# Feed-forward tiles: the up-projection one tile further ahead, and the second half of an operand's making in two pieces

## The chip, the cores and the metric

The kernel runs on one core of a Trainium2 chip. The metric is the device time of one execution in microseconds; less is better. PE is the matrix engine (TensorE), DVE the vector engine, ACT the scalar engine, POOL and SP issue transfers here.

## The reference, cut to what matters

A stream of 528 columns (16 learned tokens, 512 frames) of width 1024 goes through two layers in float32. Each has a mixer (retention in the first, latent attention in the second) and a feed-forward part; the change is in the feed-forward part alone:

```python
def swiglu(hn, w1, w3, w2):
    return (jax.nn.silu(hn @ w1) * (hn @ w3)) @ w2

for layer in range(DEPTH):
    ...
    h = h + swiglu(rmsnorm(h, norm_ffn_g[layer]), ffn_w1[layer], ffn_w3[layer], ffn_w2[layer])
```

`w1` and `w3` are 1024 x 2816, `w2` is 2816 x 1024.

## The kernel before

**Split values.** A float32 matrix is used as a high part `hi` (a copy to the matmul's type, made by ACT) and a residue `lo` (the value less `hi`, made by DVE). `split` issues the two, one after the other, and the residue waits for the copy. Each product takes three matmuls per block: `hi hi`, `hi lo`, `lo hi`.

**Tiles and periods.** The feed-forward part is a sequence of tiles (`seq`). A tile up (`Up`) takes 128 columns of `w1` and of `w3`, a tile down (`Down`) 2 x 128 columns of `w2` over one part of the 22 hidden blocks. The hidden blocks go in inner pairs: tiles up 2j and 2j+1 give pair j, of which the operand `xp` of the tiles down is made. Most tiles are multiplied in Strassen's manner, with seven products of half blocks (Q1 to Q7) for eight; the first two or three tiles up and the last part down are plain. A tile up has four blocks in each product (12 matmuls), a tile down of the first three parts three blocks (9 matmuls).

`PARTS = (3, 3, 3, 2)` are the inner pairs of the four parts. Tiles up of the first two parts run two tiles beyond those that the part needs (L1059, the `+ 2`), then come the part's four tiles down. So the sequence of 38 tiles is: up 0 to 7, down 8 to 11, up 12 to 17, down 18 to 21, up 22 to 29, down 30 to 33, down 34 to 37 (plain).

**A period** (`period(i)`, L911) issues the work of tile i = `q`, of its predecessor `prev`, and the preparation for `nxt` = i+1 and `far` = i+2. PE's order is Q1 of `q`, Q7 and Q3 of `prev`, Q5, Q2 and Q6 of `q`, Q4 of `prev`. All engines run their instructions in the order in which the code issues them. For DVE that is, in a period: the `wlo` of `group2(q)`, the `wlo4` of `group4(prev)` (names of a kind drop their digits in the profile: `wlo<-raw,whi` with 512 columns), what `hidden(i)` issues, `combine(prev)` (`b<-b,t`), two multiplications of `prev.mid` (`t<-a,r`, `t<-b,r`), `sum2(nxt)` (`raw<-raw`, L856), the `wlo` of `group(q, q.r3, ...)`, the `wlo` of `group1(nxt)`, `sum4(nxt)`, and two instructions of `prev.fin`. Each `wlo` has its `whi` on ACT, in the same order. The next period's Q1 needs the `wlo` of `group1(nxt)`.

**The operands of a pair** (`operands`, L784) are made in two steps by a generator. The first makes the parts of Q1, Q2 and Q3 and two differences `e<-e`; the second makes two more `e<-e`, and then splits all four into the parts of Q5, Q7, Q4 and Q6 (`xp<-e` on ACT, 4 x 264 columns, and the residue `xp<-e,xp` on DVE). `hidden(i)` (L1072) issues one step per period: the first step of the next pair if its values are there and a buffer is free, the second step in the period after. The list `room` holds the buffers with the period from which each is free: three at once for the first part, the same three from one period after the first part's last tile down for the second part (P13), and so on. So first steps fall on the periods 3, 5, 7, then 13, 15, 17, then 23, 25, 27, second steps on 4, 6, 8, then 14, 16, 18, then 24, 26, 28; the plain operands of the last part are made in 31 and 33.

```python
        def hidden(i):
            if rest:
                drain(rest.pop())
            elif len(ops) < len(hid) and i >= room[len(ops)][1]:
```

Of the kernel before, what the change touches and what calls it, by code (L numbers as in the profile page):

```python
# [11 lines left out]
F32 = mybir.dt.float32  # L12
# [3 lines left out]
ALU = mybir.AluOpType  # L16
# [19 lines left out]
KH = HID // P  # L36
# [11 lines left out]
PARTS = (3, 3, 3, 2)  # L48
# [3 lines left out]
Q1, Q2, Q3, Q5, Q7, Q4, Q6 = range(7)  # L52
# [10 lines left out]
def drain(steps):  # L63
    for _ in steps:
        pass
# [195 lines left out]
class Kernel:  # L261
# [522 lines left out]
    def operands(self, pool, vv, w, b12=None):  # L784


        xp = pool.tile([P, 7, 2, HT], F32R, tag="xp", name=self.name("xp"))
        (b11, b12_), (b21, b22) = ((vv[:, i, :w], vv[:, i, w : 2 * w]) for i in range(2))
        for q, z in ((slice(Q1, Q3), vv[:, :, :w]), (Q3, b22)):
            self.split(xp[:, q, 0, :w], xp[:, q, 1, :w], z)  # L790
        if b12 is not None:
            self.split(*b12, b12_)
            yield xp
        self.tt(b11, b11, b12_, ALU.subtract)
        self.tt(b12_, b22, b12_, ALU.subtract)
        if b12 is None:
            yield xp
        self.tt(b22, b22, b11, ALU.add)
        self.tt(b21, b22, b21, ALU.subtract)
        if b12 is not None:  # L800
            yield
        self.split(xp[:, Q5:, 0, :w], xp[:, Q5:, 1, :w], self.blocks(vv, w))

    @staticmethod
    def blocks(vv, w):
# [8 lines left out]
    def quads(self, seq, first, w, ready, also, hidden):  # L814
# [15 lines left out]
        def load1(q):  # L830
            q.r1 = f3(q, raw(q))
            nc.sync.dma_start(out=q.r1, in_=f3(q, q.src[:, : 2 * q.n]))

        def load3(q):
            q.r3 = f3(q, raw(q))
            nc.sync.dma_start(out=q.r3[:, 0], in_=q.part(1))

        def load2(q):
            q.r2 = f3(q, raw(q))
            if q.plain:  # L840
                nc.sync.dma_start(out=q.r2, in_=f3(q, q.src[:, 2 * q.n :]))
            else:
                nc.sync.dma_start(out=q.r2[:, 1], in_=q.part(2))
# [5 lines left out]
        def add1(q):  # L849
            nc.gpsimd.dma_start(out=q.r1[:, 1], in_=q.part(3), accum_op=ALU.add)  # L850

        def add3(q):
            nc.gpsimd.dma_start(out=q.r3[:, 0], in_=q.part(0), accum_op=ALU.add)
# [17 lines left out]
        def group1(q):  # L871
            group(q, q.r1, *((A11, A21) if q.plain else (Q1, Q5)))

        def group2(q):
            group(q, q.r2, *((A12, A22) if q.plain else (Q6, Q2)))
# [6 lines left out]
        def product(q, bank, p, first):  # L882
            wt = q.f[p]
            for k, xp in enumerate(q.xs()):
                cs = slice(k * P, (k + 1) * P)
                for i, (u, v) in enumerate(((0, 0), (0, 1), (1, 0))):
                    nc.tensor.matmul(bank, wt[u][:, cs], xp[:, p, v, :w], start=first and k == 0 and i == 0,  # L887
                                     stop=False, skip_group_check=True)

        def plain(q, j, k, of=((0, 0), (0, 1), (1, 0), (1, 1))):  # L890

            cs = slice(k * P, (k + 1) * P)
            xs = q.blocks(k)[2 * j : 2 * j + 2]
            for row, col in of:
                wt, x = q.f[((A11, A12), (A21, A22))[row][j]], xs[col]
                bank = ((q.a, q.b), (q.d, q.c))[row][col]
                for i, (u, v) in enumerate(((0, 0), (0, 1), (1, 0))):
                    nc.tensor.matmul(bank, wt[u][:, cs], x[v], start=j == 0 and k == 0 and i == 0,  # L898
                                     stop=False, skip_group_check=True)
# [11 lines left out]
        def period(i):  # L911
            q, nxt, far = (seq[j] if j < len(seq) else None for j in range(i, i + 3))
            prev = seq[i - 1] if i else None
            mixed = lambda z: z is not None and not z.plain
            on = lambda place: [f() for f in also.get((i, place), ())]
            if q:
                a, ps = self.banks[i % 2]
                q.a, (q.b, q.d, q.c), q.ps = a[:, :w], (ps[:, j, :w] for j in range(3)), ps[:, :, :w]
            if i == 0:
                load1(far)  # L920
                group1(nxt)
                if mixed(far):
                    add1(far)
                    load3(far)
                load2(far)
                if mixed(far):
                    add3(far)
                on("start")
                for k in range(len(q.xs())):
                    plain(q, 0, k)  # L930
                    plain(q, 1, k)
                    on(k)
                return
            pairs = range(len(q.xs())) if q else ()
            if mixed(q):
                product(q, q.a, Q1, True)
            elif nxt:

                for of in ((0, 1), (1, 0), (1, 1), (0, 0)) if i == 1 else ((0, 0), (0, 1), (1, 0), (1, 1)):
                    for k in pairs:  # L940
                        plain(q, 0, k, (of,))
            if q:
                group2(q)
                on("group2")
                if far and i < first:
                    load1(far)
                if mixed(q):
                    nc.scalar.copy(out=q.b, in_=q.a)
            if mixed(far):
                add1(far)  # L950
            if mixed(prev):
                group4(prev)
            if mixed(q):
                load4(q)
            hidden(i)
            if mixed(prev):
                product(prev, prev.d, Q7, False)
                product(prev, prev.b, Q3, False)
                combine(prev)
            prev.mid(prev.a, prev.b)  # L960
            on("mid")
            if mixed(nxt):
                sum2(nxt)
            if mixed(q):
                group(q, q.r3, Q7, Q3)
            if mixed(far):
                load3(far)
            if mixed(q):
                product(q, q.c, Q5, True)
            elif nxt:  # L970
                for k in pairs:
                    plain(q, 1, k)
            else:
                for row in range(2):
                    for k in pairs:
                        for j in range(2):
                            plain(q, j, k, ((row, 0), (row, 1)))
            if mixed(q):
                q.q5 = self.temp()[:, :w]
                nc.scalar.copy(out=q.q5, in_=q.c)  # L980
            if nxt:
                group1(nxt)
                if far:
                    load2(far)
                if i >= first - 1 and i + 3 < len(seq):
                    load1(seq[i + 3])
            if mixed(nxt):
                sum4(nxt)
            on("group1")
            if mixed(q):  # L990
                product(q, q.a, Q2, False)
                product(q, q.b, Q6, False)
                nc.scalar.copy(out=q.d, in_=q.b)
            prev.act()
            if mixed(prev):
                product(prev, prev.d, Q4, False)
            prev.fin(prev.ps[:, 1:3])
            if mixed(far):
                add3(far)
            on("end")  # L1000
# [12 lines left out]
    def ffn(self, layer, full):  # L1013
# [4 lines left out]
        w = HT if full else SEQ // 2  # L1018
# [37 lines left out]
        hid, ops, seq, room = [], [], [], []  # L1056
        m = 0
        for part, size in enumerate(PARTS):
            end = min(2 * sum(PARTS[: part + 1]) + 2, KH) if part < 2 else KH  # L1059
            while m < end:  # L1060
                seq.append(Up(self, a[f"w13_{layer}"][m], KD // 2, m < PLAIN[layer], m, x, hid, w))
                m += 1
            if part == 2:
                room += [(self.xp, len(seq) + 1)] * 2
            for o in range(KD // 2):
                seq.append(Down(self, a[f"w2_{layer}_{part}"][o], size, part == 3, o, ops, sum(PARTS[:part]), full))
            if part < 2:
                room += [(self.hp, len(seq) + 1)] * 3
        room = [(self.hp, 0)] * 3 + room
        rest = []  # L1070

        def hidden(i):  # L1072
            if rest:
                drain(rest.pop())
            elif len(ops) < len(hid) and i >= room[len(ops)][1]:
                make = self.operands if len(ops) < sum(PARTS[:3]) else self.plain_operands
                rest.append(make(room[len(ops)][0], hid[len(ops)], w))
                ops.append(next(rest[0]))

        self.quads(seq, PLAIN[layer], w, self.ready, also, hidden)  # L1080
        self.shut("hp", "xp", "wx")
# [325 lines left out]
```

## Time and profile before

| | us |
|---|---|
| median of 3 runs | 1473.9 (1472.87 to 1476.27) |
| the profiled execution | 1473.63 |
| its span | 1471.9 |
| feed-forward of layer 0 (in the span) | 465.90 to 819.50 |
| feed-forward of layer 1 | 1105.50 to 1455.20 |

Over the span PE is busy 97%, DVE 77%, ACT 50%, POOL 9%. In the two feed-forward stretches DVE is busy 310.33 of 353.60 us and 303.52 of 349.70 us. The share of busy time says little about which engine sets the end: PE's matmuls overlap, and DVE's share is a mean over periods with and without operands to make. So what is to be read are the few places at which a matmul starts late, and what it waited for.

### The profile page before, as it was taken

Reading aid. Unit: us, or ns where it says so; the run is one execution under the profiler, and the core shown is the slowest. Engines: PE = TensorE matmul, PEld = TensorE weight load, DVE = VectorE, ACT = ScalarE, POOL = GpSimd, SP = SyncE. Lnnn points to the kernel's source line nnn. Section 1 sums busy time; section 2 is a strip of 40 time slices with the busy share of each in tenths; the row PEclk is TensorE's granted clock in tenths of the full one; section 3 lists DMA queues with packets and bytes.
Section 4 is the critical chain, followed back from the end, with each engine's and each line's share of the span. In section 5 each row is a group of like instructions: output and inputs, shape, how many; then the busy total and the mean of one; then the engine's idle time right before and its main releaser. Section 6 shows DMA issues by size and latency. Waiting matters only on the chain.

```text
span 1471.9 us, 27735 instructions
## 1 busy us (share of the span) xinstructions
PE 1422.8 (97%) x11088; PEld 1376.7 (94%) x11088; DVE 1131.2 (77%) x1823; ACT 736.9 (50%) x1299; POOL 129.7 (9%) x170
## 2 busy tenths in 40 slices
PE   8999999999999999999999999989999999999995
PEld 8999999999999999999999989778989999999995
DVE  7665566566568998988987877567788988989876
ACT  5452442342356555555554534565556655555552
POOL 2000000000000111111110000110000112121100
PEclk9999999999999999999999999999999999999998
DMA  6213223123113767768764232311113768677651
GB/s 213 91 48 103 69 70 101 58 73 101 59 58 94 179 161 184 177 147 205 179 151 136 100 96 72 104 51 55 58 58 100 189 157 200 162 190 188 162 139 65
DMA packets 77314, 176.80 MB, mean 120 GB/s; under 512 B 8944, under 2 KB 24432, under 8 KB 77184
## 3 DMA queue, kind: packets, MB, share of 16 engines
q1 hardware_dynamic: 56592, 138.76, 29.6%
q0 software_dynamic: 20592, 36.26, 14.1%
q8 instruction: 87, 1.43, 0.4%
q14 instruction: 43, 0.35, 0.1%
HBM read 171.57 MB, written 2.10 MB: 118 GB/s over the span
## 4 chain that ended last, share of the span: by engine, by line
PE 73%; DVE 18%; ACT 3%; issue 3%; DMA 2%; DVEq 0%; ACTq 0%; POOLq 0%
PE ps L371 22%; PE b L887 16%; PE ps L373 8%; DVE wlo L331 7%; PE ps L638 6%; PE a L887 6%; PE b L898 4%; PE ps L721 2%; DVE xp L331 2%; DVE t L331 2%; DVE e L331 2%; PE ps L679 2%; PE ps L116 2%; DMA raw<-w 1%; ACT xp L335 1%
## 5 line engine op out<-in xcount | busy, mean ns | idle before, releaser
L335 ACT CAST whi<-raw 128x1024 fp32r<-128x1024 f32 (+4 forms) x402 | 347.6, 869 | 275.6 <-PE ps L371 137.8
L887 PE MATMUL b<-xp,whi 128*128 128x264 f32 (+1 forms) x2280 | 417.2, 283 | 5.6 <-DVE xp L331 3.6
L331 DVE TENSOR_TENSOR wlo<-raw,whi 128x1024 fp32r<-128x1024 f32 (+4 forms) x402 | 389.9, 995 | 40.1 <-ACT whi L335 37.3
L887 PEld LDWEIGHTS b<-xp,whi 128*128 128x128 f32 x2280 | 351.4, 188 | 7.7 <-DVE xp L331 4.4
L887 PE MATMUL b<-xp,wlo 128*128 128x264 f32 (+1 forms) x1140 | 321.7, 282 | 0.0
L371 PE MATMUL ps<-s,whi 128*128 128x264 f32 x1824 | 300.9, 287 | 9.4 <-ACT whi L335 6.7
L371 PEld LDWEIGHTS ps<-s,whi 128*128 128x128 f32 x1824 | 255.3, 190 | 11.7 <-ACT whi L335 6.7
L887 PEld LDWEIGHTS b<-xp,wlo 128*128 128x128 f32 x1140 | 214.2, 188 | 0.0
L371 PE MATMUL ps<-s,wlo 128*128 128x264 f32 x912 | 186.4, 286 | 0.0
L887 PE MATMUL a<-xp,whi 128*128 128x264 f32 (+1 forms) x912 | 170.4, 283 | 0.0
L371 PEld LDWEIGHTS ps<-s,wlo 128*128 128x128 f32 x912 | 142.4, 190 | 0.1
L887 PEld LDWEIGHTS a<-xp,whi 128*128 128x128 f32 x912 | 140.6, 188 | 0.0
L887 PE MATMUL a<-xp,wlo 128*128 128x264 f32 (+1 forms) x456 | 130.5, 286 | 8.0 <-DVE wlo L331 8.0
L850 POOL DMA_DIRECT2D raw<-w x63 | 54.6, 867 | 805.9 <-DMA raw<-w 428.6
L373 PE MATMUL ps<-s,whi 128*128 128x512 f32 x368 | 119.0, 405 | 3.4 <-ACT t L127 3.4
L638 PE MATMUL ps<-whi,s 128*128 128x256 f32 x640 | 116.5, 281 | 0.3 <-DVE s L331 0.3
L638 PEld LDWEIGHTS ps<-whi,s 128*128 128x128 f32 x640 | 99.1, 188 | 0.6 <-PE ps L118 0.3
L331 DVE TENSOR_TENSOR s<-ps,s 128x256 fp32r<-128x256 f32 (+3 forms) x88 | 46.6, 546 | 65.3 <-ACT s L335 50.8
L887 PEld LDWEIGHTS a<-xp,wlo 128*128 128x128 f32 x456 | 85.7, 188 | 11.8 <-DVE wlo L331 11.6
L638 PE MATMUL ps<-wlo,s 128*128 128x256 f32 x320 | 89.5, 280 | 0.0
L373 PEld LDWEIGHTS ps<-s,whi 128*128 128x128 f32 x368 | 68.6, 192 | 18.0 <-ACT t L127 3.5
L331 DVE TENSOR_TENSOR xp<-e,xp 128x528 fp32r<-128x528 f32 (+5 forms) x82 | 64.1, 808 | 22.9 <-ACT xp L335 22.7
(178 smaller groups left out, 2088.2 us busy)
## 6 DMA issues: line engine op xcount, KB each, us to landing
raw<-w SPq DMA_DIRECT2D x133, 256.0 KB, 3.7
raw<-w SPq DMA_DIRECT2D x49, 512.0 KB, 5.2
raw<-w POOLq DMA_DIRECT2D x78, 256.0 KB, 5.4
raw<-w SPq DMA_DIRECT2D x72, 192.0 KB, 2.9
raw<-w SPq DMA_DIRECT2D x24, 384.0 KB, 4.4
raw<-w POOLq DMA_DIRECT2D x48, 192.0 KB, 4.0
raw<-w_v SPq DMA_DIRECT2D x16, 512.0 KB, 3.7
raw<-w_g SPq DMA_DIRECT2D x16, 512.0 KB, 3.5
```

Source lines behind the costliest of these rows:

```text
L116: nc.tensor.matmul(out, x[:, qs], y[:, cs], start=t == 0, stop=t == 4 and not masked)
L331: self.nc.vector.tensor_tensor(out=out, in0=a, in1=b, op=op)
L335: self.nc.scalar.copy(out=hi, in_=src)
L371: mm(ps[:, h * 512 : h * 512 + HT], w[p], x[q][:, h * HT : (h + 1) * HT], start=s, stop=e)
L373: mm(ps[:, :SEQ], w[p], x[q], start=s, stop=e)
L638: mm(ps[:, :256], x[k][p][:, c], w[k][q], start=k == 0 and i == 0, stop=k == last and i == 2)
L679: nc.tensor.matmul(ps[:n, half * 512 : half * 512 + HT], k[d][p][:, t0 : t0 + n], q[d][s][:, half * HT : (half + 1) * HT], start=i == 0, s ...
L721: mm(out, v[j][p][:, c], s[:, c0 : c0 + HT], start=j == 0 and i == 0, stop=False)
L850: nc.gpsimd.dma_start(out=q.r1[:, 1], in_=q.part(3), accum_op=ALU.add)
L887: nc.tensor.matmul(bank, wt[u][:, cs], xp[:, p, v, :w], start=first and k == 0 and i == 0, stop=False, skip_group_check=True)
L898: nc.tensor.matmul(bank, wt[u][:, cs], x[v], start=j == 0 and k == 0 and i == 0, stop=False, skip_group_check=True)
```

## The change

Three things. The tiles up of the first two parts run three tiles beyond those that the part needs, not two. In the second step of `operands`, a `yield` stands between the copy and the residue when an inner pair's operands are made (`b12 is None`; with `b12`, at the start of a layer, nothing changes). And `hidden` is called at three places of a period: a first step is issued where it was (place 1, behind `group4`); of a second step the two differences and the copy are issued ahead of `group4` (place 0), the residue behind `prev.mid` (place 2).

```diff
@@ operands
         self.tt(b22, b22, b11, ALU.add)
         self.tt(b21, b22, b21, ALU.subtract)
+        hi, lo, vv = xp[:, Q5:, 0, :w], xp[:, Q5:, 1, :w], self.blocks(vv, w)
         if b12 is not None:
             yield
-        self.split(xp[:, Q5:, 0, :w], xp[:, Q5:, 1, :w], self.blocks(vv, w))
+        self.nc.scalar.copy(out=hi, in_=vv)
+        if b12 is None:
+            yield
+        self.tt(lo, vv, hi.bitcast(F32), ALU.subtract)
@@ period
             if mixed(far):
                 add1(far)
+            hidden(i, 0)
             if mixed(prev):
                 group4(prev)
             if mixed(q):
                 load4(q)
-            hidden(i)
+            hidden(i, 1)
             if mixed(prev):
                 product(prev, prev.d, Q7, False)
                 product(prev, prev.b, Q3, False)
                 combine(prev)
             prev.mid(prev.a, prev.b)
+            hidden(i, 2)
@@ ffn
-            end = min(2 * sum(PARTS[: part + 1]) + 2, KH) if part < 2 else KH
+            end = min(2 * sum(PARTS[: part + 1]) + 3, KH) if part < 2 else KH
@@ ffn
-        def hidden(i):
-            if rest:
-                drain(rest.pop())
-            elif len(ops) < len(hid) and i >= room[len(ops)][1]:
+        def hidden(i, place):
+
+            if rest and rest[0][0] < i:
+                if place == 0:
+                    next(rest[0][1], None)
+                if place == 2:
+                    drain(rest.pop()[1])
+            elif not rest and place == 1 and len(ops) < len(hid) and i >= room[len(ops)][1]:
                 make = self.operands if len(ops) < sum(PARTS[:3]) else self.plain_operands
-                rest.append(make(room[len(ops)][0], hid[len(ops)], w))
-                ops.append(next(rest[0]))
+                rest.append((i, make(room[len(ops)][0], hid[len(ops)], w)))
+                ops.append(next(rest[0][1]))
```

The sequence of tiles is now: up 0 to 8, down 9 to 12, up 13 to 18, down 19 to 22, up 23 to 29, down 30 to 33, down 34 to 37. First steps fall on the periods 3, 5, 7, then 14, 16, 18 (the buffers are free from 14 on), then 24, 26, 28; second steps on 4, 6, 8, then 15, 17, 19, then 25, 27, 29.

DVE in period 6 of layer 0, the second step of the second pair, as a piece of the difference (`wlo_763` is the residue `wlo4` of `group4`, `e_5861` the pair's values, `xp_6016` its operand, `b` the `combine`, `t` the `mid`):

```order
 L331 TENSOR_TENSOR wlo_6137<-raw_5945,whi_6136 128x1024
-L331 TENSOR_TENSOR wlo_763_6143<-raw_747_6014,whi_762_6142 128x512
 L331 TENSOR_TENSOR e_5861<-e_5861 128x264 x2
+L331 TENSOR_TENSOR wlo_763_6146<-raw_747_6014,whi_762_6145 128x512
+L331 TENSOR_TENSOR b_0_5379<-b_0_5379,t_6070 128x2x264
+L331 TENSOR_TENSOR t_6176<-a_0_5378,r 128x264
+L331 TENSOR_TENSOR t_6176<-b_0_5379,r 128x264
 L331 TENSOR_TENSOR xp_6016<-e_5861,xp_6016 128x4x264
-L331 TENSOR_TENSOR b_0_5379<-b_0_5379,t_6070 128x2x264
-L331 TENSOR_TENSOR t_6177<-a_0_5378,r 128x264
-L331 TENSOR_TENSOR t_6177<-b_0_5379,r 128x264
```

The residue `wlo4` went behind the two differences, and `combine` and `mid` went ahead of the operand's residue.

ACT in the same period, before:

```order
L335 CAST whi_6136<-raw_5945 128x1024
L948 COPY b_0_5377<-a_0_5376 128x264
L335 CAST whi_762_6142<-raw_747_6014 128x512
L335 CAST xp_6016<-e_5861 128x4x264
L335 CAST whi_6181<-raw_5925 128x1024
```

and after:

```order
L335 CAST whi_6136<-raw_5945 128x1024
L952 COPY b_0_5377<-a_0_5376 128x264
L803 CAST xp_6016<-e_5861 128x4x264
L335 CAST whi_762_6145<-raw_747_6014 128x512
L335 CAST whi_6181<-raw_5925 128x1024
```

The copy of the operand, which needs the two differences of DVE, went ahead of `whi4` (`whi_762`), which DVE's `wlo4` needs.

DVE in the period of the second part's first tile down, before (period 18):

```order
L331 TENSOR_TENSOR wlo_7570<-raw_7381,whi_7569 128x768
L331 TENSOR_TENSOR wlo_943_7576<-raw_927_7450,whi_942_7575 128x512
L331 TENSOR_TENSOR e_7297<-e_7297 128x264 x2
L331 TENSOR_TENSOR xp_7452<-e_7297,xp_7452 128x4x264
L331 TENSOR_TENSOR b_0_5379<-b_0_5379,t_7506 128x2x264
L331 TENSOR_TENSOR t_7610<-a_0_5378,r 128x264
L331 TENSOR_TENSOR t_7610<-b_0_5379,r 128x264
```

and after (period 19):

```order
L331 TENSOR_TENSOR wlo_7694<-raw_935_7505,whi_7693 128x768
L331 TENSOR_TENSOR e_7290<-e_7290 128x264 x2
L331 TENSOR_TENSOR wlo_958_7703<-raw_943_7575,whi_957_7702 128x512
L331 TENSOR_TENSOR b_0_5377<-b_0_5377,t_7631 128x2x264
L331 TENSOR_TENSOR t_7733<-a_0_5376,r 128x264
L331 TENSOR_TENSOR t_7733<-b_0_5377,r 128x264
L331 TENSOR_TENSOR xp_7577<-e_7290,xp_7577 128x4x264
```

Here too a second step stands in the period of the first tile down; its residue, which this period's Q5 product reads, is now the last of the seven.

## Rows read from the trace of the kernel before

**Rows 1.** Waits of PE in layer 0's feed-forward: total us, times, longest.

```profile
PE a L887 <- DVE wlo L331: 2.1, 7, 0.6
PE b L887 <- DVE xp L331: 1.8, 2, 0.9
```

**Rows 2.** The same for layer 1.

```profile
PE a L887 <- DVE wlo L331: 5.9, 10, 1.6
```

**Rows 3.** PE in time, P17's start: start us, us, instruction, count, idle before.

```profile
633.10 0.41 PE L887 MATMUL b<-xp,whi 128*128 128x264 f32 x2
...
633.46 0.41 PE L887 MATMUL a<-xp,whi 128*128 128x264 f32 x2
634.13 0.39 PE L887 MATMUL a<-xp,wlo 128*128 128x264 f32 x1 [0.26 <-DVE wlo L331]
634.36 0.40 PE L887 MATMUL a<-xp,whi 128*128 128x264 f32 x2
```

**Rows 4.** PE in time at P15's start in layer 1.

```profile
1253.69 0.39 PE L887 MATMUL a<-xp,wlo 128*128 128x256 f32 x1 [0.47 <-DVE wlo L331]
```

**Rows 5.** DVE in time, second step in P16 of layer 0.

```profile
626.61 0.89 DVE L331 TENSOR_TENSOR e<-e 128x264 f32<-128x264 f32 x2
628.65 1.26 DVE L331 TENSOR_TENSOR xp<-e,xp 128x1056 fp32r<-128x1056 f32 x1 [1.14 <-ACT xp L335]
629.82 0.71 DVE L331 TENSOR_TENSOR b<-b,t 128x528 f32<-128x528 f32 x1
...
631.12 0.68 DVE L856 SCALAR_TENSOR_TENSOR raw<-raw 128x512 f32<-128x512 f32 x1
631.72 2.36 DVE L331 TENSOR_TENSOR wlo<-raw,whi 128x1024 fp32r<-128x1024 f32 x2
```

**Rows 6.** ACT in time, the same stretch.

```profile
625.17 0.62 ACT L335 CAST whi<-raw 128x512 fp32r<-128x512 f32 x1
627.54 1.07 ACT L335 CAST xp<-e 128x1056 fp32r<-128x1056 f32 x1 [1.75 <-DVE e L331]
628.52 1.05 ACT L335 CAST whi<-raw 128x1024 fp32r<-128x1024 f32 x1
```

**Rows 7.** Chain that ended last, same stretch: start us, us, what.

```profile
627.54 1.08 ACT xp L335
```

**Rows 8.** DVE in time, P18, the first tile down.

```profile
649.37 1.26 DVE L331 TENSOR_TENSOR xp<-e,xp 128x1056 fp32r<-128x1056 f32 x1 [1.14 <-ACT xp L335]
```

**Rows 9.** PE in time, P18, its Q5 product.

```profile
648.85 0.28 PE L887 MATMUL b<-xp,wlo 128*128 128x264 f32 x1
649.39 0.39 PE L887 MATMUL b<-xp,whi 128*128 128x264 f32 x1 [0.25 <-ACT xp L335]
650.68 0.39 PE L887 MATMUL b<-xp,whi 128*128 128x264 f32 x1 [0.91 <-DVE xp L331]
650.91 0.28 PE L887 MATMUL b<-xp,wlo 128*128 128x264 f32 x1
```

**Rows 10.** DVE in time in P17, whose next tile is a tile down.

```profile
640.77 0.55 DVE L856 SCALAR_TENSOR_TENSOR raw<-raw 128x384 f32<-128x384 f32 x1
641.23 2.09 DVE L331 TENSOR_TENSOR wlo<-raw,whi 128x1024 fp32r<-128x1024 f32 x2
```

**Rows 11.** SP and POOL in time, after P16's `wlo4` (L847 is `load4`).

```profile
626.72 0.33 SPq L847 DMA_DIRECT2D raw<-w  x1
...
632.97 0.33 SPq L843 DMA_DIRECT2D raw<-w  x1
...
638.00 0.86 POOL L850 DMA_DIRECT2D raw<-w  x1 [5.88 <-DVE wlo L331]
```

**Rows 12.** PE in time, attention stage, behind its longest hole.

```profile
959.71 1.22 PE L373 MATMUL ps<-s,whi 128*128 128x512 f32 x2 [3.36 <-ACT t L127]
```

**Rows 13.** Stretches: us, PE, PEld, DVE, ACT, POOL busy (count), PEclk, DMA share, GB/s.

```profile
958.40:965.20 6.80, 5.49 (x13) 4.33 (x14) 3.92 (x12) 5.71 (x15) 3.35 (x7) 0.50 0.54 135
1455.20:1458.00 2.80, 0.04 (x2) 0.04 (x1) 2.40 (x4) 2.22 (x3) 0.00 (x0) 1.00 0.00 0
```

## The prediction

> **What bounds the kernel now.** I read the waits of the matmuls first, then the chain, then DVE, ACT and PE row by row around one repeated stall. A period is what `period(i)` issues for tile i; I write P16 for it. The clock times of the detailed rows are of the first feed-forward layer; the second repeats the pattern.
>
> TensorE is the bound nearly everywhere, and it loses time in the feed-forward layers in a few places of two kinds. In layer 0 it waits seven times for a `wlo` at the start of a period, and twice for the `xp` of a first tile down [rows 1]; in layer 1 it waits ten times for a `wlo` [rows 2]. Seven of these ten, like the seven of layer 0, follow a period that holds the second step of an inner pair. What such a stall costs: the triple of matmuls that starts at 633.10 takes 0.36 us to the start of the next, the one with the wait takes 634.36 - 633.46 = 0.90, so 0.54 us are lost [rows 3]. In layer 1 the idle time is 0.47 where it is 0.26 here [rows 3, 4], so some 0.75.
>
> Why DVE is late there: in P16, of which these are the rows, it works without a pause but for one hole. The two subtractions `e<-e` end at 626.61 + 0.89 = 627.50 and the residue `xp<-e,xp` begins at 628.65 [rows 5]: 1.15 us idle, in which ACT makes the copy `xp<-e` that the residue subtracts. That copy starts 0.04 us after the subtractions and DVE goes on 0.04 us after its end [rows 5, 6]. The chain of the program's end runs through this copy [rows 7], so the hole isn't free: from the end of P15's last matmul through DVE to the `wlo` that P17's first product needs, whatever is added or saved on DVE in P16 moves PE one for one.
>
> **The change, part by part.**
>
> *The second step in two pieces.* The same instructions with the same shapes run, so DVE's busy time stays, and only the hole can change. The idea that the code suggests is that DVE does `wlo4`, the `combine` and the two multiplications of `mid` while ACT copies. But the order on ACT puts the copy `xp<-e` ahead of `whi4`, and on DVE the next instruction after the subtractions is now the `wlo4` that needs `whi4`. So the wait isn't covered; it gets longer by one ACT instruction. Now: 0.04 + the copy of 1.07 + 0.04 = 1.15. After: 0.04, then ACT's start-to-start of that copy, 628.52 - 627.54 = 0.98, then `whi4` with 0.62, then 0.04 [rows 6]: 1.68. **+0.53 us per second step.** After the hole `combine`, `mid` and the residue follow without a wait, since what they read is long there. Bounds: 0.45 if the two ACT instructions overlap more than in these rows, 0.65 if there is no overlap at all (1.07 + 0.62 + 0.08 = 1.77); I take 0.53.
>
> Each layer has nine such second steps. Six stand after the change, as now, in a period whose next tile is a tile up (P4, P6, P15, P17, P25, P27). All six stall already, so nothing is there to absorb the 0.53: 12 x 0.53 = **+6.4 us**.
>
> *The first part's extra tile up.* The third second step falls on P8 in both kernels. P8 is now the first tile down and TensorE waits there in the Q5 product: a triple that should take the 0.36 us of [rows 3], from 648.85 to 649.21, ends at 650.91 in P18, which repeats P8 [rows 9]: 1.70 us lost. After the change P8 is a tile up, and the stall is one of the other kind, at P9's start. It is smaller than its siblings, since the next tile is a tile down with three blocks for four: `sum2` 0.55 for 0.68 and the pair of `wlo` 2.09 for 2.36 [rows 5, 10], 0.40 less. So 0.54 + 0.53 - 0.40 = 0.67 for 1.70, and 0.75 + 0.53 - 0.40 = 0.88 in layer 1, where I put the same 1.70: **-1.9 us**.
>
> *The second part.* Its operands can't run ahead, although the tiles up do: their three buffers are those of the first part, and `room` opens them one period after its last tile down, now at P14. The steps fall on P14 to P19, and the first tile down is P19: as tight as now with P13 to P18. Here the second piece does harm of its own, since the residue, which the Q5 product waits for, now stands behind `wlo4`, `combine` and `mid`. In P18 now it begins as long after the subtractions as in P16, with 1.14 us idle ahead of it [rows 8]. After: the subtractions end earlier by what `wlo4` took ahead of them, `wlo4` takes the same behind the hole, and in all the residue begins 1.68 + 1.30 = 2.98 us after the old end of the subtractions, where it was 1.15; the 1.30 is `combine` and `mid`, 631.12 - 629.82 [rows 5]. **+1.83 us** in each layer, **+3.7 us**. TensorE then stands for 0.91 + 1.83 us, and for the 0.42 that it now waits for the copy first (649.39 for 648.85 + 0.12) [rows 9]: about 3.15 us without a matmul. What comes after is shorter on DVE than on PE (three-block tiles, no operands), so it isn't made good.
>
> *The third part.* Its steps fall on P24 to P29 for P23 to P28, and the third now ends under a next tile down: +0.53 - 0.40 = +0.13, **+0.3 us** in both layers. The last part's operands are made as before, in P31 and P33.
>
> *The other queues.* The load of `raw4` waits until `wlo4` has read the buffer: on SP it is issued at 626.72 and would be at about 629.3; the load behind it shifts with it, and SP's next issue is at 632.97. The accumulating load on POOL that needs this second load has until 638.00, POOL's next [rows 11], and its data are used two periods on. I count nothing; without that cover it would be up to the 2.6 us of the shift in the periods concerned.
>
> Sum: 6.4 - 1.9 + 3.7 + 0.3 = **+8.5 us** on the profiled execution's 1473.63 us (span 1471.9), which is 0.3 us below the median of the runs: 1482.1.
>
> *The clock.* In the attention stage TensorE had 3.36 us without a matmul [rows 12]; the granted clock went to 0.50 (1.2 GHz for 2.4 GHz) before they were over and stayed there to 965.20, with 5.49 us of matmuls in those 6.80; at half speed that is 2.7 us lost. The hole of 2.8 us near the end left the clock at 1.00 [rows 13]. The holes at P19 are to be 3.15 us, between the two. I therefore take one of the two layers to lose 2.7 us: **1484.8**; none gives 1482.1, both 1487.5. The Trainium skill, "TensorE: Matmul & The Clock Gate", section "Why this matters for your kernels", warns of idle gaps of this size between bursts of matmuls, after which the clock falls back; by that rule both layers lose it and the time would be 1487.5. The two rows above agree with it on the longer hole and leave the shorter one open.
>
> **The rivals.**
> - *The hole is filled, as the two pieces suggest.* If `whi4` were ready when DVE gets to `wlo4`, DVE would gain its 1.15 us, and all fourteen stalls after second steps would go: 7 x 0.54 + 7 x 0.75 = 9.0 us. P8 gives its 1.70 twice, and P19 loses little (the residue 1.30 after the subtractions' end for 1.15): about -12 us, **1461.5**. It decides on one point: does `whi4` run on ACT before `xp<-e`? For it: ACT is idle for 1.75 us before that copy [rows 6], time enough. Against: the order of ACT's instructions, which the rows of the change show, and in this trace ACT sits in just that idle time with `whi` waiting behind the copy. I give it 0.06.
> - *The longer hole is absorbed.* If the 0.53 didn't reach TensorE, P8 would give 1.56 + 1.35 (0.54 - 0.40 for 1.70, and 0.75 - 0.40), P29 0.4 twice, and P19 would cost 3.7: about 0, **1473.6**. For it: idle time of an engine often costs nothing. Against: PE waits for DVE after every one of these periods [rows 1, 2]. I give it 0.07.
> - *The clock stays up, or falls twice*: 1482.1 and 1487.5, above; 0.27 and 0.17.
>
> **How the numbers follow.** The forecast with one fall of the clock has 0.40; with none 0.27; with two 0.17; filled 0.06; absorbed 0.07; 0.03 is left for something slower that I don't see. The likeliest gives 1484.8. The range 1479 to 1488.5 takes in the three clock cases with the bounds of the hole (0.45 to 0.65 over eighteen steps, -1.4 to +2.2 us) and leaves out the two rivals on the other side. A measurement of this kernel can tell about 0.2% (2.9 us) from no change: slower 0.87, same 0.07, faster 0.06.
>
> **What would show it.** DVE's idle time before `wlo4` with `whi4` as what ended it, about 1.68 us in each second step, and none before the residue; the stall at the start of the periods after them near 1.07 us in layer 0 and 1.28 in layer 1; no stall in P9's Q5 product; one of about 3.5 us from a matmul to the next in P19, in both layers; the granted clock there. Wrong would be: DVE going on to `wlo4` at once, or stalls as long as before.

## The result and the profile after

The changed kernel takes 1486.59 us (median of 4 runs, 1485.10 to 1488.42) where the kernel before, on the same chips, takes 1475.09 (1472.87 to 1477.14): the ratio is 1.0074, 95% interval 1.0059 to 1.0090, so it is slower, by 11.5 us or 0.7%. The profiled execution took 1487.46 us with a span of 1485.7 us; that is 13.8 us over the one of before.

Where those 13.8 us lie, from the first to the last matmul of each stage: the first feed-forward 353.6 to 359.1 us (+5.5), the second, with the matmuls of the closing norm, 353.5 to 360.3 (+6.8), the attention between them 286.1 to 287.6 (+1.5), the rest the same. The clock has a part in all three, as is seen below.

DVE in time in P17, a second step in layer 0 (compare rows 5; start us, us, instruction, count, idle before):

```profile
636.79 0.89 DVE L331 TENSOR_TENSOR e<-e 128x264 f32<-128x264 f32 x2
639.35 0.69 DVE L331 TENSOR_TENSOR wlo<-raw,whi 128x512 fp32r<-128x512 f32 x1 [1.66 <-ACT whi L335]
639.96 0.71 DVE L331 TENSOR_TENSOR b<-b,t 128x528 f32<-128x528 f32 x1
...
641.25 1.25 DVE L331 TENSOR_TENSOR xp<-e,xp 128x1056 fp32r<-128x1056 f32 x1
```

The hole is still there and has moved. The residue `xp<-e,xp` waits for nothing now, as the code intends; but `wlo4` waits 1.66 us for its `whi`, where the residue waited 1.14. What held `whi` up stands on ACT (compare rows 6):

```profile
635.68 0.36 ACT L952 COPY b<-a 128x264 f32<-128x264 f32 x1 [1.01 <-PE a L891]
637.72 1.07 ACT L803 CAST xp<-e 128x1056 fp32r<-128x1056 f32 x1 [1.67 <-DVE e L331]
638.70 1.56 ACT L335 CAST whi<-raw 128x512 fp32r<-128x512 f32 x2
```

ACT sits idle for 1.67 us in front of the copy `xp<-e`, which needs DVE's differences, and `whi4` comes behind it at 638.70 (the row's two are `whi4` and the next `whi`).

PE in time at the start of the next period, P18 (compare rows 3):

```profile
644.25 0.41 PE L891 MATMUL a<-xp,whi 128*128 128x264 f32 x2
645.43 0.39 PE L891 MATMUL a<-xp,wlo 128*128 128x264 f32 x1 [0.77 <-DVE wlo L331]
645.65 0.40 PE L891 MATMUL a<-xp,whi 128*128 128x264 f32 x2
```

The triple takes 1.40 us where 0.36 is usual: 1.04 us lost for 0.54 before. PE in time in P19, the second part's first tile down (compare rows 9):

```profile
660.15 0.28 PE L891 MATMUL b<-xp,wlo 128*128 128x264 f32 x1
660.27 0.28 PE L891 MATMUL b<-xp,whi 128*128 128x264 f32 x1
663.78 0.39 PE L891 MATMUL b<-xp,whi 128*128 128x264 f32 x1 [3.23 <-DVE xp L331]
664.01 0.29 PE L891 MATMUL b<-xp,wlo 128*128 128x264 f32 x1
```

664.01 - 660.15 - 0.36 = 3.50 us lost for 1.70. And the clock in stretches of layer 0, of the start of the attention stage and of layer 1 (us, then busy time of PE, PEld, DVE, ACT and POOL with counts, granted clock, DMA share, GB/s; compare rows 13):

```profile
660.60:663.80 3.20, 0.02 (x1) 0.02 (x1) 3.20 (x6) 0.68 (x1) 0.00 (x0) 1.00 0.80 154
665.18:668.59 3.41, 3.41 (x18) 3.41 (x17) 1.43 (x2) 1.41 (x4) 0.86 (x1) 0.50 0.61 106
829.02:832.43 3.41, 3.12 (x12) 2.70 (x11) 3.41 (x5) 2.09 (x3) 0.00 (x0) 0.50 0.40 151
1310.30:1317.13 6.83, 6.17 (x29) 6.17 (x30) 3.38 (x5) 2.54 (x5) 0.86 (x1) 0.50 0.68 164
```

Behind the hole of P19 TensorE ran at 1.2 GHz for 2.4 GHz in both layers, 3.41 and 6.83 us long. Two matmuls take 0.42 us from start to start then (1311.56 to 1311.98 in layer 1) for 0.24 at the full clock, so 43% of the busy time is lost: 1.5 and 2.7 us. The third fall, at 829.02, stands where nothing was changed; the kernel before has none there in its profile. It costs another 1.5 us or less, about what the attention stage lost.

### The profile page after: what moved, and what is told of

It is laid out like the page before. It is cut to its first block, busy times and chain, and to the rows that moved or that the text cites. A ratio compares the mean times of both kernels' runs of the same rounds, so it can differ in the third digit from the quotient of the medians.

```text
span 1485.7 us, 27735 instructions
## 1 busy us (share of the span) xinstructions
PE 1426.7 (96%) x11088; PEld 1380.9 (93%) x11088; DVE 1130.9 (76%) x1823; ACT 736.5 (50%) x1299; POOL 129.7 (9%) x170
## 4 chain that ended last, share of the span: by engine, by line
PE 74%; DVE 17%; issue 5%; ACT 3%; DMA 1%; DVEq 0%; ACTq 0%; POOLq 0%
PE ps L371 21%; PE b L891 17%; PE ps L373 8%; DVE wlo L331 7%; PE a L891 7%; PE ps L638 6%; PE b L902 4%; DVE e L331 2%; PE ps L721 2%; DVE t L331 2%; PE ps L679 2%; PE ps L116 2%; ACT whi L335 1%; DVE xp L331 1%; PE a L902 1%
## 5 line engine op out<-in xcount | busy, mean ns | idle before, releaser
L854 POOL DMA_DIRECT2D raw<-w x63 | 54.6, 867 | 739.0 <-DVE acc L331 295.5
L857 POOL DMA_DIRECT2D raw<-w x63 | 54.3, 862 | 222.2 <-DVE wlo L331 91.6
```

## The experiments

The theory: the copy in front of `whi4` on ACT makes DVE's hole longer; in P19 the residue is late besides, since it stands behind `combine` and `mid`; that hole pulls the clock down; the tile up more is a gain by itself. The rivals: the tile up more costs time; the late residue costs everywhere; the clock falls for another reason.

**One thing undone: the order on ACT.** Against the changed kernel:

```diff
@@ operands
-        if b12 is not None:
-            yield
+        yield
         self.nc.scalar.copy(out=hi, in_=vv)
@@ hidden
-                if place == 0:
+                if place < 2:
                     next(rest[0][1], None)
```

So the differences stay ahead of `group4` and the residue behind `mid`; the copy alone goes back behind `whi4`.

> The changed kernel with one thing undone: on ACT the operand's copy stands behind whi4 again (the two differences stay ahead of group4, the residue stays behind mid). Theory (ACT's order makes the hole): DVE goes on to wlo4 at once, no wait before wlo4 nor before the residue, all stalls at a period's start that follow a second step go (seven per layer, 0.54 us each in layer 0 and 0.75 in layer 1 before), the first tile down of the second part loses some 1.85 us instead of 3.5, no fall of the clock there: about 12 us below the kernel before, 1461 to 1464. Rival (the residue behind mid, or the extra tile up, is what costs): the stalls stay, and the time is at most 4 us below the changed kernel, 1482 or more.

Measured: 1463.26 us, ratio to the kernel before 0.9918 (0.9889 to 0.9948). DVE in time, a second step of layer 0:

```profile
633.37 0.90 DVE L331 TENSOR_TENSOR e<-e 128x264 f32<-128x264 f32 x2
634.18 0.68 DVE L331 TENSOR_TENSOR wlo<-raw,whi 128x512 fp32r<-128x512 f32 x1
635.18 0.72 DVE L331 TENSOR_TENSOR b<-b,t 128x528 f32<-128x528 f32 x1 [0.31 <-PE b L890]
```

The hole is gone: what is left is 0.31 us in which DVE waits for PE. And the waits of PE in layer 0 (total us, times, longest):

```profile
PE b L890 <- DVE xp L331: 1.8, 1, 1.8
PE a L901 <- DVE h L331: 0.8, 1, 0.8
PE b L890 <- ACT b L951: 0.5, 1, 0.5
PE a L890 <- DVE wlo L331: 0.2, 1, 0.2
```

Of the waits for a `wlo` one of 0.2 us is left, for 2.1 us in seven before [rows 1]; in layer 1 one of 1.5 us at the layer's start, for 5.9 in ten [rows 2]. Two neighbouring instructions of ACT, in this order or in that, are worth 23 us between the two versions: 12 below the kernel before or 11.5 above it, the falls of the clock included. One part of the expectation missed: the clock did fall in both layers, for 3.41 us, though the hole of P19 was only 2.07 us from matmul to matmul in layer 0. PE in time there, and the clock behind it:

```profile
655.80 0.28 PE L890 MATMUL b<-xp,whi 128*128 128x264 f32 x1
657.87 0.39 PE L890 MATMUL b<-xp,whi 128*128 128x264 f32 x1 [1.79 <-DVE xp L331]
```

```profile
658.40:661.80 3.40, 3.40 (x18) 3.40 (x18) 2.18 (x3) 1.11 (x2) 0.86 (x1) 0.51 0.38 94
```

**The two pieces alone**, with tiles up two ahead as before (`+ 3` back to `+ 2`).

> The two pieces as in the changed kernel, with tiles up two ahead as before. Theory: seven second steps per layer cost 0.53 more, the first tiles down of the first and of the second part lose 3.5 us each instead of 1.7: 2 x (7 x 0.53 + 2 x 1.83) = 14.7 us, so 1488, and with the clock falling after each of the four holes, at 1.5 to 2.7 us, 1494 to 1499. Rival (the extra tile up is what costs): near the kernel before, below 1480.

Measured: 1492.04 us, ratio 1.0113 (1.0086 to 1.0141): 4 us above the theory's figure without the falls and 2 us below its range with them. PE's waits in layer 0:

```profile
PE b L891 <- DVE xp L331: 6.5, 2, 3.2
PE a L891 <- DVE wlo L331: 5.7, 8, 0.8
```

Two first tiles down wait 3.2 us each, in both layers, and the clock fell behind all four holes, three times for 3.41 us and once for 6.83. In the profiled executions the two feed-forward layers are 10.0 and 10.3 us longer than in the kernel before. The attention stage is 2.5 us shorter: the fall behind its longest hole, which the kernel before has [rows 12, 13], is missing in this execution, so part of the miss is not of the change. The median is 16.7 us above the kernel before. The two pieces in this order, with the falls behind them, are all the harm.

**The tile up more alone**, the second step in one piece as before (the kernel before with `+ 3` for `+ 2`).

> The tile up more alone, with the second step in one piece as before. Theory: the stall of 1.70 us in the first part's first tile down is replaced by one of about 0.14 (layer 0) and 0.35 (layer 1), and the last tile up's stall shrinks by 0.40: 3.7 us below the kernel before, near 1470. Rival (the extra tile up costs): above the kernel before.

Measured: 1470.35 us, ratio 0.9966 (0.9948 to 0.9983). PE in time at P9's start in layer 0:

```profile
559.73 0.40 PE L887 MATMUL a<-xp,whi 128*128 128x264 f32 x2
559.99 0.39 PE L887 MATMUL a<-xp,wlo 128*128 128x264 f32 x1
560.22 0.41 PE L887 MATMUL a<-xp,whi 128*128 128x264 f32 x2
```

The triple takes 0.49 for 0.36, so 0.13 us are lost in place of the 1.70 of a first tile down. The tile up more is a gain of some 5 us here (2.5 to 7.7 by the interval), 3.7 of which were worked out.

**The whole second step early in the first tile down.** Against the changed kernel, in P19 alone (it is the one second step in the period of a tile down):

```diff
-                if place == 0:
+                if place == 0 and i < len(seq) and isinstance(seq[i], Down) and len(ops) <= sum(PARTS[:3]):
+                    drain(rest.pop()[1])
+                elif place == 0:
                     next(rest[0][1], None)
```

> The changed kernel, with the whole second step ahead of group4 where the period's tile is a tile down (once per layer, the second part's first). Theory: the matmul wait there goes from 3.5 us to about 1.1 us from a matmul to the next beyond the usual, so 2 x 2.4 us are won, and the clock stays at 1.00 there, which gives back 1.5 us (layer 0) and 2.7 us (layer 1) of the profiled execution: 1477 to 1479, with all other stalls as in the changed kernel. Rival (the falls of the clock have another cause than this hole): the clock falls as before at the same places, and the time is 1482 to 1483.

Measured: 1479.44 us, ratio 1.0022 (1.0011 to 1.0034). PE in time in P19 of layer 0, and the clock from there on, in both layers:

```profile
660.51 0.28 PE L891 MATMUL b<-xp,whi 128*128 128x264 f32 x1
661.61 0.39 PE L891 MATMUL b<-xp,whi 128*128 128x264 f32 x1 [0.82 <-DVE xp L331]
```

```profile
660.50:669.00 8.50, 7.68 (x63) 7.46 (x62) 8.30 (x13) 4.63 (x10) 0.86 (x1) 1.00 0.62 146
1305.30:1315.00 9.70, 8.83 (x74) 8.63 (x73) 9.49 (x16) 5.56 (x11) 2.32 (x3) 1.00 0.65 140
```

1.10 us from matmul to matmul for 3.51, and the clock stays at 1.00. The two feed-forward layers together are 9.2 us shorter than in the changed kernel's profile, for 9.0 expected. The median gains only 7 us and lies 0.4 above the expected range; in the profile the attention stage, where nothing was changed, is 2.4 us longer, with a fall for 6.83 us at 824 for the 3.41 of the changed kernel and one more at 933. So the late residue of P19 and the falls behind it are worth 7 to 9 us of the changed kernel's loss; with the hole the two falls are gone, in both layers of the one execution that was profiled.

**Both mended.** The copy behind `whi4` as in the first experiment, and in P19 the residue directly behind `wlo4`:

```diff
-                if place == 0:
+                if place == 1 and i < len(seq) and isinstance(seq[i], Down) and len(ops) <= sum(PARTS[:3]):
+                    drain(rest.pop()[1])
+                elif place < 2:
                     next(rest[0][1], None)
```

> The copy behind whi4 as in e1, and in the second part's first tile down the residue directly behind wlo4, ahead of combine and mid. Theory: the hole from matmul to matmul there goes from 2.07 to 1.1 us in both layers, and the clock, which fell for 3.41 us behind that hole in both layers of e1, stays at 1.00 there: 2 x (0.95 + 1.5) = 4.9 us below e1, 1458 to 1459. Rival (the clock falls have another cause): the clock falls at the same places and only 1.9 us are won, 1461 to 1462.

Measured: 1462.73 us, ratio 0.9909 (0.9892 to 0.9925). The expectation in its figure missed by 4 us, and the figure is nearer the rival's 1461 to 1462; but the rival's sign, falls of the clock at the same places, is absent. At P19 it went as expected: 1.11 and 1.15 us from matmul to matmul, the clock at 1.00 there in both layers, and layer 0 takes 347.3 us where the first experiment's takes 350.2. In this execution the gain was lost again, 1.5 us of it in the attention stage, where the clock fell at 817 us, and some at the start of layer 1; DVE in time there, and the clock a little later:

```profile
1134.56 0.69 DVE L331 TENSOR_TENSOR raw<-raw 128x512 f32<-128x512 f32 x1 [1.92 <-DMA raw<-w]
```

```profile
1148.10:1151.50 3.40, 3.40 (x19) 3.40 (x18) 3.26 (x6) 1.54 (x3) 0.00 (x0) 0.51 0.93 267
```

A load came 1.92 us late, PE then stood for 2.18 us (to 1147.02), and the clock fell. Waits of DVE for loads, 0.2 to 2 us in a place or more, are in every profile of this study and in changing places; the median of this kernel against the first experiment's (1462.73 to 1463.26, with runs of before at 1476.66 and 1475.39) therefore doesn't show the 3 us of layer 0 clearly.

**The tile up more taken away again**, in the first experiment's kernel (`+ 3` back to `+ 2`).

> e1 with tiles up two ahead as in the kernel before: what the tile up more is worth once the hole is filled. Theory: the first part's first tile down loses some 1.85 us again (2.05 from matmul to matmul), in both layers, where e1 has no stall, and the clock may fall behind it as it does in e1 behind the second part's: 3.7 to 6.7 us above e1, 1467 to 1470. Rival (the tile up more gives nothing once the order is right): as e1, 1463.

Measured: 1471.45 us, ratio 0.9971 (0.9957 to 0.9984), 8 us above the first experiment, or 7 by the distances from the kernel before, which ran slower beside this one (1476.66 for 1475.39); the expected 1467 to 1470 was too low by 1.5. PE's waits in layer 0, and the clock behind the four first tiles down of both layers:

```profile
PE b L890 <- DVE xp L331: 3.6, 2, 1.8
```

```profile
556.80:560.20 3.40, 3.40 (x18) 3.40 (x17) 1.43 (x2) 1.36 (x4) 0.86 (x1) 0.51 0.54 89
652.40:655.80 3.40, 3.40 (x18) 3.40 (x17) 1.46 (x3) 1.28 (x3) 0.36 (x1) 0.50 0.78 138
1202.00:1205.40 3.40, 3.40 (x18) 3.40 (x17) 1.43 (x2) 1.55 (x4) 0.86 (x1) 0.50 0.54 100
1294.10:1297.50 3.40, 3.40 (x18) 3.40 (x18) 1.82 (x3) 1.10 (x4) 0.86 (x1) 0.50 0.42 99
```

All four holes of some 2.05 us are followed by a fall here. But the profiled execution is the slowest of ten, 1476.66 us, with a granted clock of 0.986 over its span; the six fastest, 1468.73 to 1471.48, have 0.989 to 0.992. At 0.992 some 23 us were at the lower level, an estimate, and the closing stage alone has 13.5 in the profile; what is left is less than four falls of 3.41 us. So not every execution has all four. The tile up more keeps its worth once the hole is filled, and saves a fall per layer besides in this execution.

**The residue late, alone.** Against the changed kernel `place == 0` becomes `place == 1`: the differences and the copy stay together behind `group4`, the residue goes behind `mid`.

> Tiles up three ahead; the differences and the copy of the second step stay together behind group4 as in the kernel before, the residue alone goes behind mid. Theory: the 1.15 us of the copy are covered by combine and mid (1.30), no hole on DVE and no stall behind second steps; the second part's first tile down as in e1: the same time as e1, 1462 to 1465. Rival (the differences ahead of group4 are needed to cover the copy): part of the hole stays, 1466 or more.

Measured: 1463.44 us, ratio 0.9915 (0.9890 to 0.9940), as the first experiment. DVE in time:

```profile
633.47 0.90 DVE L331 TENSOR_TENSOR e<-e 128x264 f32<-128x264 f32 x2
634.68 0.72 DVE L331 TENSOR_TENSOR b<-b,t 128x528 f32<-128x528 f32 x1 [0.31 <-PE b L891]
```

`combine` and `mid` cover the copy by themselves; moving the differences ahead of `group4` was not needed for that. P19 is not quite as in the first experiment: its hole is broken by one matmul, with 1.66 us from that to the next in layer 0 and 1.54 in layer 1. Behind it the clock stayed up in layer 0 and fell in layer 1:

```profile
655.00:662.00 7.00, 5.48 (x43) 5.06 (x42) 5.44 (x9) 4.19 (x7) 1.70 (x2) 1.00 0.75 155
1293.90:1297.30 3.40, 3.40 (x18) 3.40 (x17) 2.17 (x3) 1.10 (x2) 0.36 (x1) 0.50 0.67 130
```

## Why the prediction was right

- **The hole of DVE.** Forecast 1.68 us before `wlo4`, with `whi4` as what ends it, for 1.15 before the residue; measured 1.66, and nothing before the residue. The first experiment changes the order on ACT alone, with the copy behind `whi4`, and the hole is gone; the last, with the same order on ACT, has none either.
- **The stalls that follow.** Forecast 1.07 us in layer 0 and 1.28 in layer 1; measured 1.04, and in layer 1 1272.27 - 1270.67 - 0.35 = 1.25.
- **P8.** Forecast 0.67 and 0.88 at P9's start for 1.70 in the Q5 product; measured 0.66 (560.63 to 561.65, less 0.36) and 0.84 (1210.17 to 1211.36, less 0.35), and no wait in the Q5 product. The third experiment shows the gain of the tile up more alone.
- **P19.** Forecast 3.53 us lost (1.70 + 1.83); measured 3.50 in layer 0. The hole without a matmul was to be 3.15 us and is 3.23. The fourth experiment takes most of it away (1.10 us from matmul to matmul).
- **The other queues.** The load that was to shift by 2.6 us did (P17's `load4` at 640.07, behind a `wlo4` that ends at 640.04), and the next issue of SP is at 644.26, of POOL, after the load that depends on it, at 650.83. It held nothing up: DVE has no wait for a load in this layer's feed-forward.
- **The sum.** Without the clock, layer 0 is 5.5 - 1.5 = 4.0 us longer and layer 1 6.8 - 2.7 = 4.1: 8.1 us for a forecast of 8.5. In layer 1 the fit is in part luck, since two differences outside the sum nearly cancel there: the stall of PE at the layer's start, behind loads that come late, is 2.17 us for 1.56, with another of 0.20 ahead of it, and a stall of 0.51 at 1326.32 in the kernel before, behind a load that came 1.67 us late, is gone.
- **The clock.** This is the step that was mis-sized. I let one of the two holes pull it down, between a row with a fall behind 3.36 us and one read as without a fall behind 2.8. Both did, at 1.5 and 2.7 us for the one 2.7: the case with two falls, which had only 0.17. A third fall of 1.5 us or less stands in the attention stage of this execution, which the sum had no term for. That is some 3 us more than I had, and with the 0.4 less of the sum it makes the 2.7 by which the profiled 1487.46 lies over 1484.8. The medians differ by 11.5 us for the 11.2 forecast; so close a fit is luck, since they hold falls whose number changes from one execution to the next. And the row with 2.8 us was misread. Its stretch ends at 1458.00 with the hole itself [rows 13]; a little later in the same trace stands

```profile
1460.20:1463.20 3.00, 0.00 (x0) 0.00 (x0) 2.96 (x2) 0.00 (x0) 0.00 (x0) 0.50 0.00 0
```

The clock did fall, 1.1 us after the end of TensorE's last matmul (at 1459.10). Whether the 2.8 us set that off or the idle time of the end can't be told, but the row was no sign that such a hole leaves the clock up; holes of 2.05 us were enough in the experiments.
- **The rivals.** The filled hole was ruled out by the order of ACT's instructions, and its price was near: 12 us below the kernel before worked out, 12.1 between the medians once that order is changed. In part this is luck: between the profiled spans it is 9.4 (1471.9 to 1462.5), since P19 lost 2.06 us for the 1.85 of the rival, and the clock fell behind it in both layers. The absorbed hole fell with the stalls at 1.04 us.

## What to carry to other kernels

When work is moved to fill a wait, look at every engine that it touches, not only at the one that waits: the filler on DVE here needed an instruction of ACT, and that one had been put behind the very copy that was to be hidden. A moved step is ordered by its last consumer too; where the result is needed in the same period, as in P19, putting its last piece behind other work costs what that work takes. Undoing one part at a time pays: of this change's three parts one (the tile up more) and a half (the late residue) are gains, and without the rest they give 0.9915 of the kernel before.

## What the runs showed of the hardware

- In the feed-forward layers the clock fell to 0.50 behind holes of PE much shorter than the 3.36 us of the row that I had. In P8 and P19 of the profiled executions all six holes of 3.51 to 3.53 us from matmul to matmul (two in the changed kernel, four in the second experiment) and all six of 2.02 to 2.08 (two in the first, four in the sixth) were followed by a fall, of 3.41 us mostly and of 6.83 in two cases; none was behind the four of 1.10 to 1.15 us. In the changed kernel such a fall cost 1.5 and 2.7 us beside the hole.
- The length of a hole does not decide it alone. Behind the attention stage's hole of 3.36 us without a matmul the clock fell in seven of the nine profiles (not in the second and the sixth experiment's); behind the same stage's hole of 2.06 us (2.46 from matmul to matmul) in three, the fourth's, the sixth's and the seventh's, and not in the kernel before.
- Single falls come and go where nothing was changed: at the start of the attention stage, between 817 and 829 us, six of the nine profiles have one (the changed kernel's and those of the third to the seventh experiment), the kernel before has none. What sets them off there I did not try. They go with the scatter between executions of one kernel: of the nineteen of the kernel before that ran beside the first four experiments, the fastest, 1470.94 us, had a granted clock of 0.994 over its span, the slowest, 1481.06, of 0.989. A difference of 0.005 over some 1475 us is 7 of those 10 us, an estimate.
